# Experts of a mixture layer: the second product in four column quarters at once, the next expert's first product ahead of it, the sums by halves, the overflow path in the middle

## The chip, the cores and the metric

The kernel runs on one core of one Trainium2 chip. The metric is device time in microseconds (us) of one execution; the profile is of one execution of the same program. TensorE is the matrix engine (PE in the rows, PEld its weight loads), VectorE is DVE, ScalarE is ACT, GpSimd is POOL, and SyncE (SP) issues the weight loads.

## The reference

Two transformer blocks over 256 tokens of width 1024, all in float32. Block 1 is a mixer of gated linear attention and retention, followed by a mixture of 32 experts in 4 groups; block 2 has a gated recurrence mixer, two convolutional feed-forward layers and latent attention. The change is in the mixture of experts:

```python
def _hierarchical_moe(u, rg_w, rg_b, re_w, re_b, wg, wu, wd):
    ...
    g_idx = jnp.argmax(g_logits, axis=-1)
    ...
    top_v, top_i = lax.top_k(e_logits, TOP_K_IN_GROUP)
    weights = g_w * jax.nn.softmax(top_v, axis=-1)
    expert_ids = g_idx[:, None] * EXPERTS_PER_GROUP + top_i
    ...
    def run_block(args):
        e, tok, w = args
        xb = t[tok]
        hid = jax.nn.silu(xb @ wg[e]) * (xb @ wu[e])
        return ((hid @ wd[e]).astype(jnp.float32) * w[:, None])
    ...
    y = jnp.zeros((n, D), jnp.float32).at[slot_tok].add(outs.reshape(n_slots, D))
```

Each token goes to 2 of 32 experts. An expert's weights are two 1024 x 512 matrices (gate and up) and one 512 x 1024 matrix (down): 6 MiB, 192 MiB for all 32.

## The kernel before

All weights come through one stream of loads on SyncE's queue (`_load`, L302 to L309, issue line L306). One load fills one slot: a tile `w` of 128 x 2048 float32, 1 MiB. The slots are one pool (`sp`, tag "S") of `NS = 20`, and larger intermediate tensors (`x`, the hidden state of all tokens, among them) take slots of the same pool. `plan_loads` counts beforehand how many slots are alive at each point of the program and puts each load at the earliest point at which a slot is free, with two slots left over. Behind that, a load waits on the chip for what last used its slot, and for the load that went eight places ahead of it: the loads take eight completion semaphores in turn. Outside the experts every weight tile is split into a high and a low part (L324 on ScalarE, L325 on VectorE) and multiplied in three products (L359 to L361); the experts' weights are used as they come.

The mixture of experts is `moe` (from L982). After the routing, the experts are handled in 8 groups of 4; each expert has 32 token places (`CAP`). `moe_gather` (L1147) makes the token matrix of one group: 0/1 matrices on VectorE, 16 products `xg` (L1165), two scalings (L1168). `moe_weights` (L1172) makes `ct`, the weighted matrix from places to tokens. For each expert, `expert_hidden` (L1186) multiplies the 32 gathered tokens with the gate and up weights: for each of 8 row tiles, four products of 32 x 256 (L1193) that go to the four 32-column strips of the array and to the four 32-row strips of one bank `gu`. Then come Silu (L1196), the product with the up half (L1197), a transposition (L1198) and its copy (L1200). `expert_down` (L1203) multiplies with the down weights: two products of 32 x 512 for each of 4 row tiles (L1207), into rows 32 e to 32 e + 31 of two banks `ys`, so that all eight of an expert lie in the same 32-column strip. In the trace a float32 product is two matmul instructions. After the fourth expert of a group, `moe_combine` (L1210) copies the two banks to SBUF (L1215) and adds them to the tokens with four products (L1217) into four banks `acc`, which collect all 8 groups.

After the last group, `acc` is added to `x` (L1113) into `xn`. Then stands the overflow path: the largest number of tokens that any expert has (`ci`) is read into a register of every engine (L1118), and `If(n_max > CAP)` (L1119) encloses a loop that handles tokens beyond 32 places with weights loaded into two slots `ow`. With these inputs the path is skipped: the engines jump over it. Behind it, `hgrn` (from L1220) transposes `xn` (`tp`, L471), makes its high and low parts (L460, L462) and starts its first product `gf` (L359).

On each engine the instructions stand in one order, fixed when the program is built. What is inside the `If` is a unit of its own, and nothing moves from one side of it to the other.

## Time and profile before

| | |
|---|---|
| time, median of 3 runs | 1517.41 us (1516.98 to 1517.58) |
| span of the profiled execution | 1516.6 us, 0.8 us below the median |
| TensorE busy | 1435.2 us, 95% |
| VectorE busy | 792.6 us, 52% |
| ScalarE busy | 624.9 us, 41% |
| read from memory | 367.24 MB |
| experts: first product to last product | 414.4 to 870.1 us |

Matmuls are pipelined and their ends are modelled, so a busy TensorE is not TensorE at its peak. A wait is put down to what ended last. "SPq" is SyncE's queue: idle time there is a load that was held back. The times of the profiled execution count from its first instruction.

### The profile page before, as it was taken

The page shows a single profiled execution, that of the slowest core. Times are in us where ns is not written, and L with a number is a line of the kernel's source. Part 1 is how long each engine was busy: PE and PEld are TensorE (multiplying, and loading weights), DVE is VectorE, ACT ScalarE, POOL GpSimd, SP SyncE. Part 2 cuts the span into 40 slices and gives each one's busy share as a digit, 9 for nine tenths or more (in the row PEclk, how much of TensorE's full clock was granted, in tenths as well). Part 3 has the DMA queues.
Part 4 walks back from the last instruction along what each step waited for, and adds up shares of the span by engine and source line. Part 5 has one row for each costly group of instructions (what it writes and reads, how often), then busy time and mean ns, then how long its engine had stood idle before and what let it go on. Part 6 is the DMA issues. An engine that isn't in the chain of part 4 may idle for free. (4 is left out here: it accounts for less than half of the span.)

```text
span 1516.6 us, 24847 instructions
## 1 busy us (share of the span) xinstructions
PE 1435.2 (95%) x10158; PEld 1061.3 (70%) x10158; DVE 792.6 (52%) x1738; ACT 624.9 (41%) x1374; POOL 26.5 (2%) x31
## 2 busy tenths in 40 slices
PE   7999999999899988989989899999999998999998
PEld 7898878877743333333333298779999986799997
DVE  5987475655400000000000079878777767687794
ACT  5645444644200000000000085466656676565672
POOL 0000000000000000000000000000000001000000
PEclk9999999999899999999999999899999999999999
DMA  8335432586799999999999923456554214565500
GB/s 355 130 112 210 179 138 87 201 323 235 295 418 421 421 421 420 420 421 421 421 421 421 408 69 124 152 223 226 191 174 140 72 54 194 200 220 195 192 1 29
DMA packets 53529, 369.96 MB, mean 244 GB/s; under 512 B 6161, under 2 KB 7057, under 8 KB 9634
## 3 DMA queue, kind: packets, MB, share of 16 engines
q1 hardware_dynamic: 53410, 368.31, 62.1%
q8 instruction: 82, 1.34, 0.3%
q14 instruction: 37, 0.30, 0.1%
HBM read 367.24 MB, written 1.05 MB: 243 GB/s over the span
## 5 line engine op out<-in xcount | busy, mean ns | idle before, releaser
L325 DVE TENSOR_TENSOR wl<-w,wh 128x512 fp32r<-128x512 f32 (+2 forms) x644 | 403.9, 666 | 75.1 <-ACT wh L324 56.5
L324 ACT ACTIVATE wh<-w 128x512 fp32r<-128x512 f32 (+2 forms) x644 | 347.8, 613 | 158.6 <-PE u L360 65.8
L1207 PE MATMUL y<-w,t 128*32 128x512 f32 x512 | 227.4, 597 | 10.7 <-ACT t L1200 10.7
L359 PE MATMUL u<-xh,wh 128*128 128x256 f32 x704 | 199.4, 283 | 0.0
L360 PE MATMUL u<-xl,wh 128*128 128x256 f32 x704 | 199.2, 283 | 0.0
L361 PE MATMUL u<-xh,wl 128*128 128x256 f32 x704 | 199.1, 283 | 0.0
L1197 DVE TENSOR_TENSOR t<-t,gu 128x128 f32<-128x128 f32 x32 | 9.2, 288 | 315.5 <-ACT t L1196 315.5
L1207 PEld LDWEIGHTS y<-w,t 128*32 128x32 f32 x512 | 53.9, 110 | 160.7 <-issue 143.3
L1193 PE MATMUL gu<-w,t 128*32 128x256 f32 x2048 | 144.4, 382 | 0.0
L359 PE MATMUL gt<-wh,xh 128*128 128x512 f32 (+1 forms) x352 | 139.4, 396 | 0.0
L359 PEld LDWEIGHTS u<-xh,wh 128*128 128x128 f32 x704 | 134.9, 192 | 0.9
L360 PEld LDWEIGHTS u<-xl,wh 128*128 128x128 f32 x704 | 134.9, 192 | 0.8
L360 PE MATMUL gt<-wl,xh 128*128 128x512 f32 (+1 forms) x352 | 135.2, 384 | 0.0
L361 PE MATMUL gt<-wh,xl 128*128 128x512 f32 (+1 forms) x352 | 135.2, 384 | 0.0
L361 PEld LDWEIGHTS u<-xh,wl 128*128 128x128 f32 x704 | 134.9, 192 | 0.0
L1196 ACT ACTIVATE t<-gu 128x128 f32<-128x128 f32 x32 | 8.9, 278 | 252.2 <-PE gu L1193 252.2
L1193 PEld LDWEIGHTS gu<-w,t 128*32 128x32 f32 x2048 | 68.9, 109 | 56.9 <-issue 20.2
L359 PE MATMUL gf<-xh,wh 128*128 128x256 f32 x320 | 93.4, 292 | 1.7 <-ACT wh L324 1.7
L360 PE MATMUL gf<-xl,wh 128*128 128x256 f32 x320 | 91.9, 287 | 0.0
L361 PE MATMUL gf<-xh,wl 128*128 128x256 f32 x320 | 91.5, 287 | 0.0
L359 PEld LDWEIGHTS gt<-wh,xh 128*128 128x128 f32 x352 | 66.8, 190 | 12.8 <-ACT wh L324 0.5
L360 PEld LDWEIGHTS gt<-wl,xh 128*128 128x128 f32 x352 | 66.8, 190 | 12.9 <-issue 1.0
(394 smaller groups left out, 2144.8 us busy)
## 6 DMA issues: line engine op xcount, KB each, us to landing
w<-in_ex_gu SPq DMA_DIRECT2D x128, 1024.0 KB, 19.0
w<-in_ex_d SPq DMA_DIRECT2D x64, 1024.0 KB, 19.6
w<-in_w_in SPq DMA_DIRECT2D x44, 1024.0 KB, 5.4
w<-in_f_up SPq DMA_DIRECT2D x44, 1024.0 KB, 4.9
w<-in_f_dn SPq DMA_DIRECT2D x22, 1024.0 KB, 4.8
w<-in_hg_in SPq DMA_DIRECT2D x16, 1024.0 KB, 15.7
w<-in_br_ret SPq DMA_DIRECT2D x8, 1024.0 KB, 6.4
w<-in_br_gla SPq DMA_DIRECT2D x4, 1024.0 KB, 5.5
```

The lines of the kernel that those rows point to most:

```text
L324: self.nc.scalar.activation(h[:, a], r[:, a], AF.Copy)
L325: self.nc.vector.tensor_sub(l[:, a], r[:, a], h[:, a].bitcast(F32))
L359: mm(out, lh, rh, start=first, stop=False)
L360: mm(out, lh, rl, start=False, stop=False)
L361: mm(out, ll, rh, start=False, stop=last)
L1193: nc.tensor.matmul(b[32 * j:32 * j + 32, 0:256], xg[k // 4][:, (k % 4) * P + 32 * e:(k % 4) * P + 32 * e + 32], w[:, o:o + 256], start=k = ...
L1196: nc.scalar.activation(sg, b[:, 0:128], AF.Silu)
L1197: nc.vector.tensor_mul(hd, sg, b[:, 128:256])
L1207: self.nc.tensor.matmul(ys[c][32 * e:32 * e + 32, :], hT[:, 32 * j:32 * j + 32], ed[j // 2][:, o:o + 512], start=j == 0, stop=j == 3)
```

## The change

The second product is split by columns into four quarters of 256 instead of two halves of 512. For each row tile, the four quarters go to the four 32-row strips of one bank `y` and so to the four 32-column strips of the array, as the first product does. The strips are then copied to rows 32 e to 32 e + 31 of two SBUF tiles `Y`, two copies on VectorE and two on ScalarE for each expert; the copies of whole banks in `moe_combine` go. The transposition is a function of its own (`expert_turn`), and the second product of an expert is written behind the first product of the next one (`finish(prev)`); the stream of loads is ordered the same way. `moe_weights` moves to the end of its group. The sums over groups are made in two halves: groups 0 to 3 are added to `x` into `xn`, groups 4 to 7 to `xn`. The overflow path (`moe_rest`) stands between the halves, and takes three slots instead of two. The pool has 21 slots instead of 20, a pool of 512-wide tiles has 6 buffers instead of 5, and two 16-wide tiles have 2 buffers instead of 3. `x` is freed only at the end, so that `x` and `xn` are both alive in the second half. Comments and docstrings are gone throughout.

```diff
-NS = 20
+NS = 21
...
-    BUFS = {"t512": 5, "t384": 3, "t256": 7, "t128": 7}
+    BUFS = {"t512": 6, "t384": 3, "t256": 7, "t128": 7}
...
-        ms = self.small(16, "rsm", bufs=3)[:, :n]
+        ms = self.small(16, "rsm")[:, :n]
...
-        t = self.small(16, "rst", bufs=3)[:, :n]
+        t = self.small(16, "rst")[:, :n]
...
-        for e in range(NE):
-            for i in range(4):
-                self.add(("gu", e, i), A["ex_gu"][e, i], False)
-            for i in range(2):
-                self.add(("ed", e, i), A["ex_d"][e, i], False)
+        for e in range(NE + 1):
+            if e < NE:
+                for i in range(4):
+                    self.add(("gu", e, i), A["ex_gu"][e, i], False)
+            if e:
+                for i in range(2):
+                    self.add(("ed", e - 1, i), A["ex_d"][e - 1, i], False)
...
-        b = self.bank("cn")
-        mm(b[:, 0:32], one, A32[:, 0:32], start=True, stop=False)
-        mm(b[:, 0:32], one, A32[:, 32:64], start=False, stop=True)
-        cm, ci = sm(1), self.small(1, "ci", I32, bufs=1)
-        nc.vector.tensor_reduce(cm, b[:, 0:32], axis=AX.X, op=ALU.max)
-        nc.vector.tensor_copy(ci, cm)
-
-        nxt = (oh[1], self.moe_weights(oh[0], W3[:, :, 0:4]))
-        acc = [self.bank("cb") for _ in range(4)]
+        xn = None
+
+        def finish(last):
+
+            (g, e), hid, Y, oh = last
+            hT = self.expert_turn(*hid)
+            ed = [self.get(("ed", 4 * g + e, i)) for i in range(2)]
+            self.expert_down(hT, e, ed, Y)
+            self.free(*ed)
+            if e == 3:
+                ct = self.moe_weights(oh, W3[:, :, 4 * g:4 * g + 4])
+                self.moe_combine(ct, Y, acc, g % 4 == 0, g % 4 == 3)
+
+        nxt, prev = oh, None
         for g in range(8):
+            if g % 4 == 0:
+                acc = [self.bank("cb") for _ in range(4)]
             cur = nxt
-            ys = [self.bank("y"), self.bank("y")]
+            Y = [self.t512(), self.t512()]
             for e in range(4):
                 gu = [self.get(("gu", 4 * g + e, i)) for i in range(4)]
-                hT = self.expert_hidden(cur[0], e, gu.__getitem__)
+                hid = self.expert_hidden(cur[1], e, gu.__getitem__)
                 self.free(*gu)
-                ed = [self.get(("ed", 4 * g + e, i)) for i in range(2)]
-                self.expert_down(hT, e, ed, ys)
-                self.free(*ed)
-                if e == 1 and g < 7:
-                    a = slice(4 * g + 4, 4 * g + 8)
-                    oh = self.moe_gather(R3[:, :, a])
-                    nxt = (oh[1], self.moe_weights(oh[0], W3[:, :, a]))
-            self.moe_combine(cur[1], ys, acc, g == 0, g == 7)
-
-        xn = self.S("xn")
-        for c in range(2):
-            for t in range(2):
-                a = slice(t * D + c * 512, t * D + (c + 1) * 512)
-                nc.vector.tensor_add(xn[:, a], x[:, a], acc[2 * t + c])
-
-        ow = [self.S("ow") for _ in range(2)]
+                if prev:
+                    finish(prev)
+                prev = (g, e), hid, Y, cur[0]
+                if e == 1 and g % 4 < 3:
+                    nxt = self.moe_gather(R3[:, :, 4 * g + 4:4 * g + 8])
+            if g == 0:
+                b = self.bank("cn")
+                mm(b[:, 0:32], one, A32[:, 0:32], start=True, stop=False)
+                mm(b[:, 0:32], one, A32[:, 32:64], start=False, stop=True)
+                cm, ci = sm(1), self.small(1, "ci", I32, bufs=1)
+                nc.vector.tensor_reduce(cm, b[:, 0:32], axis=AX.X, op=ALU.max)
+                nc.vector.tensor_copy(ci, cm)
+            if g % 4 == 3:
+                finish(prev)
+                prev, base = None, xn or x
+                xn = xn or self.S("xn")
+                for c in range(2):
+                    for t in range(2):
+                        a = slice(t * D + c * 512, t * D + (c + 1) * 512)
+                        nc.vector.tensor_add(xn[:, a], base[:, a], acc[2 * t + c])
+            if g == 3:
+                self.moe_rest(nc.values_load(ci[0:1, 0:1], min_val=0, max_val=T), R32, W32, xn,
+                              [sm(n) for n in (64, 8, 8)])
+                nxt = self.moe_gather(R3[:, :, 16:20])
+        self.free(x)
+        self.x = xn
+
+    def moe_rest(self, n_max, R32, W32, xn, tmp):
+
+        nc, A = self.nc, self.A
+        ow = [self.S("ow") for _ in range(3)]
         for w in ow:
             nc.vector.memset(w[:, 0:1], 0.0)
-        n_max = nc.values_load(ci[0:1, 0:1], min_val=0, max_val=T)
+        q = [ow[2][:, i * 512:(i + 1) * 512] for i in range(4)]
         with self.tc.If(n_max > CAP):
+            Rr, Rg, Wg = tmp
+            nc.vector.tensor_copy(Rr, R32)
             with self.tc.For_i(1, T // CAP, 1):
-                nc.vector.tensor_scalar(R32, R32, -float(CAP), None, op0=ALU.add)
...
+                    oh, xg = self.moe_gather(Rg3, q[0:2])
+                    Y = q[2:4]
                     for e in range(4):
                         def load(name, i):
                             nc.gpsimd.dma_start(ow[i % 2], A[name][ds(g * 4 + e, 1), i].rearrange("o p f -> p (o f)"))
...
-                        hT = self.expert_hidden(oh[1], e, lambda i: load("ex_gu", i))
-                        self.expert_down(hT, e, [load("ex_d", i) for i in range(2)], ys)
-                    acc = [self.bank("cb") for _ in range(4)]
-                    self.moe_combine(ct, ys, acc, True, True)
+                        hT = self.expert_turn(*self.expert_hidden(xg, e, lambda i: load("ex_gu", i)))
+                        self.expert_down(hT, e, [load("ex_d", i) for i in range(2)], Y)
+                    ct = self.moe_weights(oh, Wg3)
                     for c in range(2):
+                        b2 = [self.bank("cb") for _ in range(2)]
                         for t in range(2):
+                            nc.tensor.matmul(b2[t], ct[:, t * P:(t + 1) * P], Y[c], start=True, stop=True)
                             a = slice(t * D + c * 512, t * D + (c + 1) * 512)
-                            nc.vector.tensor_add(xn[:, a], xn[:, a], acc[2 * t + c])
-        self.free(x, *ow)
...
+        return b, hd
+
+    def expert_turn(self, b, hd):
+        nc = self.nc
         nc.tensor.transpose(b[:, 256:384], hd, self.ident)
         hT = self.small(128, "t128")
         nc.scalar.copy(hT, b[:, 256:384])
         return hT
 
-    def expert_down(self, hT, e, ed, ys):
+    def expert_down(self, hT, e, ed, Y):
+
+        nc = self.nc
+        b = self.bank("y")
         for j in range(4):
-            for c in range(2):
-                o = (j % 2) * 1024 + c * 512
-                self.nc.tensor.matmul(ys[c][32 * e:32 * e + 32, :], hT[:, 32 * j:32 * j + 32],
-                                      ed[j // 2][:, o:o + 512], start=j == 0, stop=j == 3)
-
-    def moe_combine(self, ct, ys, acc, first, last):
-        """Four experts' outputs, weighted, to their tokens."""
-        nc = self.nc
+            for c in range(4):
+                o = (j % 2) * 1024 + c * 256
+                nc.tensor.matmul(b[32 * c:32 * c + 32, 0:256], hT[:, 32 * j:32 * j + 32], ed[j // 2][:, o:o + 256],
+                                 start=j == 0, stop=j == 3)
+        for c in range(4):
+            dst, src = Y[c // 2][32 * e:32 * e + 32, (c % 2) * 256:(c % 2 + 1) * 256], b[32 * c:32 * c + 32, 0:256]
+            if c % 2:
+                nc.scalar.copy(dst, src)
+            else:
+                nc.vector.tensor_copy(dst, src)
+
+    def moe_combine(self, ct, Y, acc, first, last):
+
         for c in range(2):
-            y = self.t512()
-            nc.scalar.copy(y, ys[c])
             for t in range(2):
-                nc.tensor.matmul(acc[2 * t + c], ct[:, t * P:(t + 1) * P], y, start=first, stop=last)
-
```

The order of the instructions follows from this code. TensorE at the first experts: `gu` is an expert's bank of the first product, `y` the second product, `w` the weight slots, `t` small tiles. Before:

```order
L1193 MATMUL gu_3752<-w_3250,t_477_3716 32x256 x8
L1193 MATMUL gu_3752<-w_3322,t_477_3716 32x256 x8
L1198 MATMUL gu_3752<-ident,t_491_3786 128x128
L1207 MATMUL y_3750<-w_3382,t_492_3790 32x512
L1207 MATMUL y_3751<-w_3382,t_492_3790 32x512
...
L1193 MATMUL gu_3812<-w_3448,t_475_3705 32x256 x8
```

And now, at the same place:

```order
L1217 MATMUL gu_3740<-w_3250,t_476_3699 32x256 x8
L1217 MATMUL gu_3740<-w_3252,t_476_3699 32x256 x8
L1217 MATMUL gu_3785<-w_3324,t_475_3698 32x256 x8
L1217 MATMUL gu_3785<-w_3384,t_475_3698 32x256 x8
L1217 MATMUL gu_3785<-w_3448,t_476_3699 32x256 x8
L1217 MATMUL gu_3785<-w_3450,t_476_3699 32x256 x8
L1226 MATMUL gu_3740<-ident,t_487_3774 128x128
L1238 MATMUL y_3833<-w_3452,t_495_3823 32x256 x8
L1238 MATMUL y_3833<-w_3454,t_495_3823 32x256 x8
```

The second expert's first product (`gu_3785`) has moved ahead of the first expert's transposition, and the second product is 16 products of 256 columns into one bank instead of 8 of 512 into two.

SyncE's queue at the middle of the experts, where the overflow path now stands. The names in brackets are what a load waits for: DMAHW0 to DMAHW7 are the eight completion semaphores, DMASW those of GpSimd's loads in the overflow path. Before, the same queue crosses the path among the loads of `hgrn`:

```order
L306 DMA w_5916<-in_hg_in 128x2048 [waits DMAHW7_49,PE_49]
L306 DMA w_5918<-in_hg_in 128x2048 [waits DMAHW0_49,PE_49]
L1118 TENSOR_LOAD ci_3735 [waits DVE_49]
L1119 COMPARE_AND_BRANCH
...
L1118 ISA x2
L306 DMA w_6399<-in_hg_in 128x2048 [waits DMAHW1_49,PE_49]
```

And now:

```order
L306 DMA w_4983<-in_ex_gu 128x2048 [waits DMAHW5_49,PE_49]
L306 DMA w_4985<-in_ex_gu 128x2048 [waits DMAHW6_49,PE_49]
L1130 TENSOR_LOAD ci_4031 [waits DVE_49]
L1143 COMPARE_AND_BRANCH
...
L1130 ISA x2
L306 DMA w_5448<-in_ex_d 128x2048 [waits DMAHW7_49,PE_49]
L306 DMA w_5450<-in_ex_d 128x2048 [waits DMAHW0_49,PE_49]
L306 DMA w_5452<-in_ex_gu 128x2048 [waits DMASW7_49,DMAHW1_49,DVE_49,PE_49]
L306 DMA w_5491<-in_ex_gu 128x2048 [waits DMAHW2_49,DMASW6_49]
L306 DMA w_5493<-in_ex_gu 128x2048 [waits DVE_49,DMAHW3_49,PE_49,Activation_49]
L306 DMA w_5495<-in_ex_gu 128x2048 [waits DMAHW4_49,PE_49]
```

The crossing has moved from behind the experts' last loads to the 110th of their 192 loads, which is the last gate and up load of the 19th expert; the two loads behind it take two slots that were left free, the next three the slots `ow`.

TensorE at the end of the experts: `cb` are the four products of `moe_combine`, `tp` the transpositions of `hgrn`. Before:

```order
L1217 MATMUL cb_3747<-t_892_5980,t_833_5618 128x512
L1217 MATMUL cb_3749<-t_892_5980,t_833_5618 128x512
L1118 TENSOR_LOAD ci_3735
L1119 COMPARE_AND_BRANCH
...
L1119 UNCONDITIONAL_BRANCH
L471 MATMUL tp_6324<-ident,xn_5984 128x128 x2
```

And now:

```order
L1238 MATMUL y_6711<-w_6543,t_944_6709 32x256 x8
L1204 MATMUL ct_6735<-ident,t_946_6732 128x128 x2
L1238 MATMUL y_6711<-w_6545,t_944_6709 32x256 x8
L1251 MATMUL cb_5442<-t_899_6410,t_948_6738 128x512
L1251 MATMUL cb_5444<-t_899_6410,t_948_6738 128x512
L1251 MATMUL cb_5443<-t_900_6411,t_948_6738 128x512
L1251 MATMUL cb_5445<-t_900_6411,t_948_6738 128x512
L471 MATMUL tp_6763<-ident,xn_5044 128x128 x2
```

The branch between the last sums and the first transposition is gone, and only half of the last expert's second product stands behind its last load (`w_6545`). Before and after the experts TensorE's rows are the same but for a few neighbours that changed places.

## Rows read from the trace of the kernel before

**Rows 1.** The page: busy time of TensorE.

```profile
PE 1435.2 (95%) x10158; PEld 1061.3 (70%) x10158; DVE 792.6 (52%) x1738; ACT 624.9 (41%) x1374; POOL 26.5 (2%) x31
```

**Rows 2.** Windows: busy per engine, granted clock, share of the DMA engines, GB/s.

```profile
430.00:850.00 420.00, 380.81 (x2650) 150.51 (x2651) 25.48 (x80) 27.13 (x81) 0.00 (x0) 1.00 1.01 421
```

**Rows 3.** Waits of TensorE from 430 to 850 us: total, times, longest.

```profile
PE gu L1198 <- DVE t L1197: 19.8, 26, 0.8
...
PE gu L1198 <- DMA w<-in_ex_gu: 1.6, 2, 0.8
```

**Rows 4.** Timeline of TensorE: start, length, line, tiles, count.

```profile
407.25 6.57 PE L1165 MATMUL xg<-t,x 128*128 128x128 f32 x32 [1.05 <-DVE t L1157]
413.66 0.31 PE L1085 MATMUL cn<-t,cst 128*128 128x32 f32 x2
...
414.37 3.66 PE L1193 MATMUL gu<-w,t 128*32 128x256 f32 x64
...
520.58 3.70 PE L1217 MATMUL cb<-t,t 128*128 128x512 f32 x8
...
528.65 0.33 PE L1198 MATMUL gu<-ident,t 128*128 128x128 f32 x1 [0.78 <-DVE t L1197]
...
859.37 7.05 PE L1207 MATMUL y<-w,t 128*32 128x512 f32 x16 [0.35 <-ACT t L1200]
```

**Rows 5.** Timeline of ScalarE: the first bank's copy in groups 1 and 2.

```profile
519.83 0.59 ACT L1215 COPY t<-y 128x512 f32<-128x512 f32 x1 [6.29 <-PE y L1207]
...
578.31 0.59 ACT L1215 COPY t<-y 128x512 f32<-128x512 f32 x1 [6.28 <-PE y L1207]
```

**Rows 6.** SyncE's issues: experts' loads 19, 20, 192, and eight later.

```profile
400.87 0.33 SPq L306 DMA_DIRECT2D w<-in_ex_gu  x1
415.50 0.33 SPq L306 DMA_DIRECT2D w<-in_ex_gu  x1
...
832.23 0.33 SPq L306 DMA_DIRECT2D w<-in_ex_d  x1
...
852.09 0.33 SPq L306 DMA_DIRECT2D w<-in_hg_in  x1
```

**Rows 7.** Waits on SyncE's queue from 430 to 850 us.

```profile
SPq L306 <- DMA w<-in_ex_gu: 161.2, 84, 3.4
```

**Rows 8.** Timeline at the end of the experts: TensorE, VectorE, ScalarE.

```profile
866.35 3.70 PE L1217 MATMUL cb<-t,t 128*128 128x512 f32 x8
...
870.09 0.69 DVE L1113 TENSOR_TENSOR xn<-x,cb 128x512 f32<-128x512 f32 x1 [0.17 <-PE cb L1217]
...
874.11 3.45 PE L471 MATMUL tp<-ident,xn 128*128 128x128 f32 x16 [4.06 <-PEq L1119]
...
874.81 0.90 ACT L460 ACTIVATE xh<-tp,wc 128x256 fp32r<-128x256 f32 x2 [7.76 <-PE tp L471]
...
879.10 0.36 PE L359 MATMUL gf<-xh,wh 128*128 128x256 f32 x1
```

**Rows 9.** The overflow path's branch (L1119): ns min/median/max, first and last start.

```profile
L1119 SPq COMPARE_BRANCH  x1: 50/50/50, 853.0 to 853.0; - x1
...
L1119 PEldq COMPARE_BRANCH  x1: 6103/6103/6103, 867.7 to 867.7; - x1
```

**Rows 10.** Copies on ScalarE out of PSUM: ns min/median/max.

```profile
L1200 ACT COPY t<-gu x32: 266/266/267, 419.1 to 859.1; 128x128 f32<-128x128 f32 x32
...
L1215 ACT COPY t<-y x16: 586/586/587, 463.6 to 866.5; 128x512 f32<-128x512 f32 x16
```

**Rows 11.** Windows ahead of the experts: TensorE busy, granted clock (third from the end).

```profile
400.00:405.00 5.00, 1.05 (x10) 0.97 (x9) 4.03 (x31) 0.97 (x3) 0.00 (x0) 0.78 1.01 421
405.00:410.00 5.00, 3.95 (x19) 3.82 (x20) 1.77 (x10) 0.00 (x0) 0.00 (x0) 0.50 0.98 411
410.00:412.50 2.50, 2.50 (x13) 2.50 (x13) 0.69 (x1) 0.00 (x0) 0.00 (x0) 0.50 0.03 13
```

**Rows 12.** TensorE's longest wait in total after the experts, 872 us to the end.

```profile
PE sd L565 <- DVE lv L541: 4.2, 4, 2.1
```

More of the change, by code (lines that the diff above doesn't have):

```diff
@@ L1159, in moe_gather @@
         wn = self.p("nffn")
-        xg = []
+        xg = xg or [self.t512() for _ in range(2)]
         for d0 in range(0, 8, 4):
@@ L1201, in expert_hidden @@
         return hT
-    def expert_down(self, hT, e, ed, ys):
+    def expert_down(self, hT, e, ed, Y):
+        nc = self.nc
+        b = self.bank("y")
         for j in range(4):
-            for c in range(2):
-                o = (j % 2) * 1024 + c * 512
-                self.nc.tensor.matmul(ys[c][32 * e:32 * e + 32, :], hT[:, 32 * j:32 * j + 32],
-                                      ed[j // 2][:, o:o + 512], start=j == 0, stop=j == 3)
-    def moe_combine(self, ct, ys, acc, first, last):
-        nc = self.nc
+            for c in range(4):
[9 more added lines that the diff above has]
+    def moe_combine(self, ct, Y, acc, first, last):
         for c in range(2):
-            y = self.t512()
-            nc.scalar.copy(y, ys[c])
             for t in range(2):
-                nc.tensor.matmul(acc[2 * t + c], ct[:, t * P:(t + 1) * P], y, start=first, stop=last)
+                self.nc.tensor.matmul(acc[2 * t + c], ct[:, t * P:(t + 1) * P], Y[c], start=first, stop=last)
     def hgrn(self):
```

15 lines of the change are left out of this document (6 added, 9 removed).

## The prediction

> **What bounds the kernel now.** I read the page first. TensorE is busy 1435.2 of 1516.6 us [rows 1], which invites the thought that any matmul time saved is time won. So I next cut out the stretch that the change touches, by windows. From 430 to 850 us TensorE is busy 381 of 420 us, but the DMA engines are busy all the time (share 1.01) at 421 GB/s [rows 2]. Two resources run near their limit together, and the question is which one waits. TensorE waited for a landing load 1.6 us in all of these 420 us; its larger wait is for VectorE inside an expert, 19.8 us [rows 3]. The loads waited for other loads, 161 us on the gate and up weights alone [rows 7], since each needs the one eight places ahead to have landed. So the loads do not starve TensorE, and they have no pause either.
>
> The rates show why. TensorE needs 58.5 us for a group of four experts (578.31 - 519.83) [rows 5]. The loads of a group are 24 tiles of 1.0486 MB; at 421 GB/s [rows 2] a tile is 2.49 us and a group 59.8 us. The two are within 1.3 us. TensorE begins at 414.4 with a store of tiles: the 19th load went out at 400.87 and the 20th had to wait until 415.50, when TensorE had freed the first slot [rows 6]. Because both run at one rate, most of that store is still unread at the end. The last expert load went out at 832.23, and the load eight places behind it, which needs its landing, at 852.09 [rows 6]: landed at 852.1. The last second product ends at 866.4 (859.37 + 7.05) [rows 4], 14.3 us later. That lag is what a faster TensorE can remove; the 437 us of loading are not.
>
> **The change, part by part.** *Second product.* An expert's 16 instructions of 512 columns take 7.05 us, 0.43 us each, one behind the other. The first product's 64 instructions of 256 columns, in the four strips, take 3.66 us, 0.057 us each [rows 4]. The new second product has that form: 32 x 0.057 = 1.8 us, 5.2 us less for each expert. An expert is then 3.7 + 0.3 + 1.8 = 5.8 us, the gather 6.6 us and the sums 3.7 us [rows 4]; with some 4 us of waits a group takes TensorE 38 us against 59.8 us of loads. The store is used up after about two groups, and from there each tile is multiplied as it lands. The 5.2 us are hidden behind the loads except at the end.
>
> *Start.* The count of tokens (0.3 us alone, at 413.66) and `ct` leave the path to the first product at 414.37 [rows 4]: 0.7 us. The 21st slot lets one more tile land before the experts start, one of 173 that took from 415.50 to 852.09 [rows 6]: 2.5 us. The last landing comes 3.2 us earlier, at 848.9. This needs the loads to stay without a pause.
>
> *Middle.* Let T be the landing of the 16th expert's last tile. Behind it SyncE has 10 more loads before the branch, then five into slots that are free or freed by the sums. The 16th load behind T needs a slot that the 17th expert's first product frees. TensorE ends its second product and copies at T + 2, the sums at T + 6.5 (4.4 us, below). Its branch took 6.1 us from 867.7, SyncE's 0.05 us [rows 9]; the gather is 6.6 us [rows 4]. So the slot is free at about T + 20. The 16th load may go when the 8th has landed, T + 20, and the DMA engines run dry only when the 15th has, T + 37. I price the middle at nothing: the eight loads in flight cover it, with 17 us to spare, and beyond that each us costs one. `xn` and the third slot `ow` leave at least 14 tiles ahead; eight fill the queue.
>
> *End.* After the last landing only half of one second product is left, 16 x 0.057 = 0.9 us, say 1.1 with its start, where 14.3 us stood: 13.2 us less. Behind it the copies of 32 x 256 are new, and no row has this shape. ScalarE's copies of 128 x 128 and 128 x 512 took 0.27 and 0.59 us [rows 10]; two in turn on each engine are 0.5 to 1.2 us, and I take 0.8, nearer to the small one as the rows are 256 long. With the hand-over that is 1.0. Products and sums then take what they took, 866.35 to 870.78, 4.4 us [rows 8]. Before, 4.4 us stood between the last second product and the end of the sums as well (866.4 to 870.8), since the first bank's copy overlapped it. So the end loses 1.0 us here.
>
> *The branch.* From the end of the sums (870.78) to the first `xh` (874.81) are 4.0 us, of which TensorE's branch explains the wait of 4.06 us [rows 8]. It goes. In its place ScalarE's `xh` stands behind one small operation on VectorE and one on ScalarE (the `lb` values, now after the sums), 0.7 us together by my guess from nothing to 1.5. Gain 3.3 us. From `xh` to the first `gf` (879.10) I leave the 4.3 us: the first tiles of `hg_in` land at about 851 and 854, well ahead.
>
> *Clock.* [...] Fed tile by tile, TensorE will have many short waits, and the clock may be low at the end. At that level the last half product, sums and transpositions would cost 0.9 + 3.7 + about 1 = 5.6 us more. With the clock high the sum is 3.2 + 13.2 - 1.0 + 3.3 = 18.7 us; low throughout, 13.1. I take 16.3, between the two, as no row shows this pattern. [...]
>
> *The rest.* Outside the experts TensorE's order is the same, and its largest wait there is 4.2 us [rows 12]: the extra slot and the two smaller buffers can move at most a few us, which I put at nothing, with 3 us either way.
>
> **The sum.** 1516.6 - 16.3 = 1500.3 us of span; the median stood 0.8 us above the span, so 1501 us.
>
> **The rivals.** *TensorE still behind at the end* (17%): the clock is low so often that TensorE enters the last group with a lag of half a group's gather and sums. Then the end gains 5 us rather than 13, and the time is 1509. For it: the low clock doubles a group to 76 us, more than the 59.8. Against: a TensorE that lags is busy without pause, and the fully busy stretch from 410 to 412.5 is the last one at the low level [rows 11].
>
> *Nothing* (6%): the loads bound before and after, so that neither product nor branch matters; 1514 to 1520. For it: the DMA engines are already full [rows 2]. Against: the 14.3 us between the last landing and the last product, and the branch, are no loading time.
>
> *Slower* (5%): the clock stays low through the experts. Eight groups at 76 us are 608 us where 456 stood (414.4 to 870.1), so about 1669 us. It decides from the point where a group takes more than 59.8 + 16.3 / 8 = 61.8 us, that is with the clock low for 63% of TensorE's work.
>
> *All of the saving counts* (1%): 32 x 5.2 = 166 us, 1351. It would need loads faster than the 421 GB/s.
>
> *The extra slot helps elsewhere too* (11%): loads in block 2 come earlier and a few us of TensorE's waits there go; 1495 to 1497.
>
> **How the numbers follow.** The case of the sum has 60%, at 1496 to 1506: its two clocks give 1498.7 and 1504.3, and 2 us for the rest. I widen to 1495 to 1509, which takes in the extra slot and a TensorE somewhat behind, and leaves out the tails on both sides. A difference under 0.2% (3 us) could not be told from no change. Faster: 60 + 17 + 11 + 1 = 89%; same 6%; slower 5%.
>
> **What would show it.** Right: DMA share 1.0 from 420 us on without a gap at the middle; TensorE's waits for the experts' loads grow from 2 us to over 100; the last `ed` tile lands near 849 and the sums end 6 to 10 us later; no wait on the branch ahead of `tp`; `gf` begins near 863. Wrong: a dip in GB/s where the branch now stands, second products longer than 2 us at the high clock, or an experts' stretch in which TensorE never waits for loads.

## The result, and the profile after

| | before | after |
|---|---|---|
| median of the runs, us | 1517.2 (1514.7 to 1517.6) | 1501.9 (1501.1 to 1504.2) |
| profiled execution: time, span, us | 1517.4, 1516.6 | 1504.2, 1502.5 |

The ratio is 0.9897, with a 95% interval from 0.988 to 0.9915: 15.3 us less, within the predicted range and 1 us above the predicted time. The profiled execution of after is the slowest of its four, 2.3 us above the median; where those microseconds lie is shown below.

Three views of after answer to [rows 1], [rows 2] and [rows 3]: the page's busy time, the windows, and TensorE's waits from 430 to 850 us (line, waited for: us in total, times, longest).

```profile
PE 1341.5 (89%) x10670; PEld 1040.7 (69%) x10670; DVE 822.4 (55%) x1807; ACT 637.4 (42%) x1423; POOL 26.5 (2%) x31
```

```profile
core 0: us, PE busy (x) PEld busy (x) DVE busy (x) ACT busy (x) POOL busy (x), PEclk, DMA share, GB/s
405.00:410.00 5.00, 2.02 (x8) 1.91 (x9) 3.87 (x28) 1.49 (x2) 0.00 (x0) 0.52 1.01 426
430.00:850.00 420.00, 303.22 (x3173) 134.32 (x3162) 53.16 (x149) 37.74 (x126) 0.00 (x0) 0.79 1.01 421
630.00:635.00 5.00, 2.79 (x13) 2.82 (x14) 1.43 (x7) 0.00 (x0) 0.00 (x0) 0.55 1.01 416
850.00:870.00 20.00, 15.56 (x118) 11.54 (x119) 13.65 (x31) 12.61 (x30) 0.00 (x0) 1.00 1.01 420
```

```profile
PE gu L1217 <- DMA w<-in_ex_gu: 64.5, 63, 2.7
PE y L1238 <- DMA w<-in_ex_d: 20.7, 18, 10.7
...
PE xg L1189 <- PEq L1143: 4.3, 1, 4.3
```

TensorE is busy 94 us less, and the time falls by 15. The stretch from 430 to 850 us is as full of loads as before, 421 GB/s; TensorE's busy time in it fell from 381 to 303 us, and waits for the experts' tiles, 85 us, stand where 1.6 us stood. The branch, now in the middle, holds TensorE 4.3 us, and the window from 630 to 635 us, in which it ends, shows no dip of the DMA engines: share 1.01, 416 GB/s.

The time was won behind the last landing. The timeline of the end, on SyncE, TensorE, VectorE and ScalarE (start, us, engine, line, what ended the idle time before), answers to [rows 6] and [rows 8]:

```profile
833.11 0.33 SPq L306 DMA_DIRECT2D w<-in_ex_d  x1
852.98 0.33 SPq L306 DMA_DIRECT2D w<-in_hg_in  x1
...
852.96 1.07 PE L1238 MATMUL y<-w,t 128*32 128x256 f32 x16 [0.96 <-DMA w<-in_ex_d]
854.96 3.70 PE L1251 MATMUL cb<-t,t 128*128 128x512 f32 x8 [0.93 <-ACT t L1243]
858.50 1.93 PE L471 MATMUL tp<-ident,xn 128*128 128x128 f32 x16
...
864.30 0.39 PE L359 MATMUL gf<-xh,wh 128*128 128x256 f32 x1 [0.50 <-ACT wh L324]
...
854.10 0.42 DVE L1245 COPY t<-y 32x256 f32<-32x256 f32 x1 [3.26 <-PE y L1238]
...
858.70 0.69 DVE L1128 TENSOR_TENSOR xn<-xn,cb 128x512 f32<-128x512 f32 x1 [0.17 <-PE cb L1251]
...
854.55 0.36 ACT L1243 COPY t<-y 32x256 f32<-32x256 f32 x1 [2.14 <-DVE t L1245]
...
860.70 1.57 ACT L460 ACTIVATE xh<-tp,wc 128x256 fp32r<-128x256 f32 x4 [1.00 <-DMA w<-in_hg_in]
```

The last expert load went out at 833.11; the issue eight places behind it, at 852.98, marks its landing. The last half product starts at that moment and ends at 854.03: a lag of 1.05 us where 14.3 stood. No wait on the branch stands ahead of `tp`. Block 2's first product `gf` starts at 864.30 instead of 879.10.

The start of an execution varies (`rk` starts between 403.9 and 407.5 us in four executions of what is one program up to there, below), so the terms are best counted from the routing's product `rk`, which comes ahead of all that was moved. It started at 404.75 before and at 406.94 after, as the timelines of TensorE show, first before, then after:

```profile
404.75 0.61 PE L1058 MATMUL rk<-t,cst 128*128 128x32 f32 x2 [3.95 <-issue]
...
406.94 0.61 PE L1060 MATMUL rk<-t,cst 128*128 128x32 f32 x2 [3.95 <-issue]
```

| stretch | before, us | after, us | won |
|---|---|---|---|
| `rk` to the last landing | 852.09 - 404.75 = 447.3 | 852.98 - 406.94 = 446.0 | 1.3 |
| last landing to end of the last second product | 14.3 | 1.05 | 13.3 |
| to the end of the sums | 4.4 | 859.39 - 854.03 = 5.4 | -1.0 |
| to the first `xh` | 4.0 | 860.70 - 859.39 = 1.3 | 2.7 |
| to the first `gf` | 4.3 | 3.6 | 0.7 |
| sum | 474.3 | 457.4 | 17.0 |

The start took 2.2 of these 17.0 us in this execution, and block 2, from `gf` to the end of the span, 0.7 (637.5 and 638.2), which leaves the 14.1 us by which the spans differ. Block 2 took 635.0 to 641.2 us in the fourteen profiles of this document, so a difference of a few us between two single executions can lie there.

### The profile page after: what moved, and what is told of

It is laid out like the page before. It is cut to its first block, busy times and chain, and to the rows that moved or that the text cites. A ratio compares the mean times of both kernels' runs of the same rounds, so it can differ in the third digit from the quotient of the medians.

```text
span 1502.5 us, 25968 instructions
## 1 busy us (share of the span) xinstructions
PE 1341.5 (89%) x10670; PEld 1040.7 (69%) x10670; DVE 822.4 (55%) x1807; ACT 637.4 (42%) x1423; POOL 26.5 (2%) x31
## 3 DMA queue, kind: packets, MB, share of 16 engines
HBM read 367.24 MB, written 1.05 MB: 245 GB/s over the span
## 4 chain that ended last, share of the span: by engine, by line
PE 54%; DMA 27%; DVE 8%; ACT 3%; issue 1%; POOL 0%; SPq 0%; ACTq 0%; POOLq 0%; DVEq 0%
DMA w<-in_ex_gu 19%; DMA w<-in_ex_d 7%; PE u L359 6%; PE u L360 6%; PE u L361 6%; PE gt L360 4%; PE gt L361 4%; PE gt L359 4%; PE acc L360 3%; PE acc L359 3%; PE acc L361 3%; DVE wl L325 3%; PE gu L1217 1%; PE op L359 1%; PE op L360 1%; PE op L361 1%
## 5 line engine op out<-in xcount | busy, mean ns | idle before, releaser
L1217 PE MATMUL gu<-w,t 128*32 128x256 f32 x2048 | 155.9, 446 | 65.7 <-DMA w<-in_ex_gu 64.5
L1217 PEld LDWEIGHTS gu<-w,t 128*32 128x32 f32 x2048 | 64.4, 122 | 154.0 <-DMA w<-in_ex_gu 102.6
L1238 PE MATMUL y<-w,t 128*32 128x256 f32 x1024 | 92.7, 500 | 25.1 <-DMA w<-in_ex_d 22.7
L1245 DVE COPY t<-y 32x256 f32<-32x256 f32 x64 | 26.8, 418 | 145.2 <-PE y L1238 132.2
L1243 ACT COPY t<-y 32x256 f32<-32x256 f32 x64 | 23.3, 364 | 136.7 <-DVE t L1245 136.7
L1238 PEld LDWEIGHTS y<-w,t 128*32 128x32 f32 x1024 | 33.8, 133 | 66.2 <-issue 32.4
```

What stands on the lines that cost most here:

```text
L1217: nc.tensor.matmul(b[32 * j:32 * j + 32, 0:256], xg[k // 4][:, (k % 4) * P + 32 * e:(k % 4) * P + 32 * e + 32], w[:, o:o + 256], start=k = ...
L1238: nc.tensor.matmul(b[32 * c:32 * c + 32, 0:256], hT[:, 32 * j:32 * j + 32], ed[j // 2][:, o:o + 256], start=j == 0, stop=j == 3)
L1243: nc.scalar.copy(dst, src)
L1245: nc.vector.tensor_copy(dst, src)
```

## Experiments

Twelve kernels ran, with four to ten measured executions each. The four of a batch ran on one chip beside the kernel before, whose medians were 1518.0, 1517.5 and 1518.5 us.

### The changed kernel once more

No edit. It is the anchor for the others, and tells whether the late start is the change's.

> The changed kernel once more, unaltered, as the anchor of this chip and for a second profile. Theory (the gain is the lag behind the last landing, some 13 us, plus some 3 us of branch): 1502 us. In the first profile the experts began 2.2 us later than before; if that was the start of that one execution (a load of the first block that landed 1.3 us later), this profile shows the first gather at about 405 us; if the change made it (smaller buffers, another order of loads), at 407 us again.

Measured: 1500.7 us (1499.6 to 1504.6), ratio 0.9882 (0.9864 to 0.9899). Its profile started late again, and so this run alone says nothing. Two kernels below, with the branch at the end and with the strips in turn, have the same instructions in the same order up to `rk` on every engine. The timeline at `rk` of the anchor:

```profile
407.54 0.61 PE L1060 MATMUL rk<-t,cst 128*128 128x32 f32 x2 [3.95 <-issue]
```

and of the kernel with the branch at the end:

```profile
403.86 0.60 PE L1060 MATMUL rk<-t,cst 128*128 128x32 f32 x2 [3.96 <-issue]
```

With the strips in turn (405.61) and the first profile of after (406.94) these are four executions of one and the same program up to there, and they reach `rk` between 403.9 and 407.5 us. The late start belongs to the execution, not to the change. Counted from `rk`, the anchor's last landing (853.23) comes after 445.7 us.

### Quarters, order ahead, neither

The second product's strips one after another, with the next expert's first product still ahead:

```
-        for j in range(4):
-            for c in range(4):
+        for c in range(4):
+            for j in range(4):
```

> The changed kernel with the second product one strip after another (the four instructions of a strip behind each other), so that its strips do not run at once; the next expert's first product still goes ahead. The second product should take about 6.9 us instead of 1.9. A group is then 4 x (3.7 + 6.9 + 0.3) + 6.6 + 3.7 + 0.3 = 54 us and about 1 of waits, 55, against 60 us of loads: eight groups end at 416 + 440 = 856, some 3 us behind the last landing. Theory (removed lag): 1505 us, with 1502 to 1508. Rival 1 (only the concurrent quarters remove the lag): 1514. Rival 2 (the branch is the whole gain): 1502, with no lag to be seen in the records of the end.

Measured: 1503.5 us (1503.2 to 1505.5), ratio 0.9901 (0.9886 to 0.9917). That is within the expected 1502 to 1508, but not for the expected reason: the second product took 4.7 us and not 6.9, as the third kernel of this section shows, so TensorE stayed well ahead of the loads. The lag was 4.6 us (856.21 - 851.62).

The quarters kept, each expert finished before the next one's first product, and the loads in that order:

```
-                if prev:
-                    finish(prev)
-                prev = (g, e), hid, Y, cur[0]
+                finish(((g, e), hid, Y, cur[0]))
```

> The changed kernel with each expert finished before the next one's first product, and the loads in that order; the quarters stay. TensorE then waits for the hidden values once for each expert, 1.2 us more of 32 times, so that a group is 38 + 5 = 43 us, still far under the 60 us of loads. Theory: 1502, the order ahead is worth nothing here. Rival (the order ahead carries the gain): 1507 or more.

Measured: 1500.8 us (1499.2 to 1504.1), ratio 0.9888 (0.9871 to 0.9905). The order ahead is worth nothing in the time beside the quarters, as the theory said, though the lag without it was 2.7 us (852.94 - 850.25).

Both edits at once:

> Both undone: the second product one strip after another and no first product ahead; the overflow path stays in the middle and the 21 slots stay. A group of TensorE is as long as before, 58.5 us, against 60 us of loads, so the store of tiles is not used up and the lag of some 13 us comes back. Theory: 1502 + 13 = 1515, with 1511 to 1516. Rival (branch and extra slot are the gain): 1502.

Measured: 1504.1 us (1502.3 to 1509.6), ratio 0.9903 (0.9887 to 0.9919), far from the 1515 expected. The edit did not do what it was meant to, as the timeline of this kernel shows (the 32 instructions of one product, and the landing and last product at the end):

```profile
501.41 1.05 PE L1233 MATMUL y<-w,t 128*32 128x256 f32 x4 [0.35 <-ACT t L1223]
502.76 3.71 PE L1233 MATMUL y<-w,t 128*32 128x256 f32 x28
...
853.77 0.33 SPq L306 DMA_DIRECT2D w<-in_hg_in  x1
...
854.79 4.09 PE L1233 MATMUL y<-w,t 128*32 128x256 f32 x28
```

Taken in turn, the strips still needed 4.7 us and not 6.9 (1.05 and 3.71, with two products `ct` between them). TensorE was faster than the loads: its last wait for one, 1.70 us, ended at 848.78, and it was in the first four instructions of the last product when the last tile landed at 853.77. What stands behind that, 5.1 us, is most of one product, since its first strip already needs both tiles. So this run tests no slow TensorE. It shows that a second product of 4.7 us is nearly as good as one of 1.9.

### The old second product in the changed kernel

The next two put the old product back, 16 instructions of 512 columns into the group's two banks with one copy each, everything else staying. First without the order ahead:

```
+        for j in range(4):
+            for c in range(2):
+                o = (j % 2) * 1024 + c * 512
+                self.nc.tensor.matmul(ys[c][32 * e:32 * e + 32, :], hT[:, 32 * j:32 * j + 32],
+                                      ed[j // 2][:, o:o + 512], start=j == 0, stop=j == 3)
```

> The changed kernel with the second product as it was before (16 instructions of 512 columns, 7.05 us, into the group's two banks, copied once for each group) and no first product ahead; overflow path in the middle, 21 slots and the sums by halves stay. The strips in turn took only 4.6 us a product, so that run left TensorE at 52 us a group; here it needs 58.5 again, against 60 us of loads, and the branch in the middle, which now has no idle time to hide in, costs it some 5 us more. Theory (the lag behind the last landing is set by TensorE's time for a group, and vanishes below some 55 us): the last second product ends near 871, gf begins near 880, 1517 us, with 1513 to 1519. Rival 1 (the branch's place and the slots are the gain): 1502 to 1505. Rival 2 (the lag comes back, and the branch's place still gains its 3 us): 1514.

Measured: 1513.9 us (1510.6 to 1518.2), ratio 0.9973 (0.9961 to 0.9984). Two groups' first copies on ScalarE, the last landing, the last product and the gather behind the branch in this kernel:

```profile
519.60 0.59 ACT L1240 COPY t<-y 128x512 f32<-128x512 f32 x1 [6.29 <-PE y L1234]
577.38 0.58 ACT L1240 COPY t<-y 128x512 f32<-128x512 f32 x1 [6.29 <-PE y L1234]
...
849.57 0.33 SPq L306 DMA_DIRECT2D w<-in_hg_in  x1
...
856.34 7.05 PE L1234 MATMUL y<-w,t 128*32 128x512 f32 x16 [0.35 <-ACT t L1227]
...
643.54 2.28 PE L1188 MATMUL xg<-t,x 128*128 128x128 f32 x19 [2.16 <-issue]
```

A group takes 57.8 us again and the lag is back: 863.39 - 849.57 = 13.8 us. The kernel with the quarters and no order ahead, 1500.8 us, differs from this one by the product and its copies alone: they are worth 13 us. This is the theory's mechanism, but rival 2's time. The branch in the middle did hold TensorE, for 4.25 us and then 2.16 us more within the gather. The two groups around it took 117.4 us where two others take 115.6, and from the first `gu` to the last product TensorE needed 449.4 us, no longer than the 452 before. Its `gf` started 6.4 us earlier than before and its span was only 2.7 shorter. Block 2 lost the rest; 2.3 us of it are one wait of TensorE (`sd`, L565) for nothing that the profile names, the others I have not followed.

Then with the order ahead:

> The changed kernel with the second product as it was before (7.05 us), and the next expert's first product still ahead of it. What goes is TensorE's wait for the hidden values, 19.8 us of seven groups, and the one for their transposed copy, 9.9 us: a group is some 54.3 us instead of 58.5. Theory: just below the knee, TensorE catches up with the loads near the end, and behind the last landing half an old product, 3.5 us, stands instead of 1.1: 1503.5 us, with 1502 to 1508. Rival (only the quarters remove the lag): 1513 or more.

Measured: 1509.8 us (1505.9 to 1512.7), ratio 0.9954 (0.994 to 0.9967), 6 us worse than expected. The timeline of this kernel, group, landing and the last two products:

```profile
520.29 0.59 ACT L1245 COPY t<-y 128x512 f32<-128x512 f32 x1 [5.86 <-PE y L1239]
576.09 0.59 ACT L1245 COPY t<-y 128x512 f32<-128x512 f32 x1 [5.86 <-PE y L1239]
...
850.18 0.33 SPq L306 DMA_DIRECT2D w<-in_hg_in  x1
...
842.69 13.87 PE L1239 MATMUL y<-w,t 128*32 128x512 f32 x32 [0.32 <-DMA w<-in_ex_d]
```

A group takes 55.8 us here, and TensorE catches up only in the last group. Then two old products, 13.87 us, stand one behind the other from 842.69 while their tiles land 5 us apart: the lag is 856.56 - 850.18 = 6.4 us and not 3.5. The group was expected at 54.3 us, and the branch in the middle, which the expectation left out, held TensorE for 4.25 and 2.41 us. The profiled execution is the fastest of five whose others reach 1512.7; why they spread I have not shown, and the lag of the others is not known.

### The branch at the end

```
-            if g == 3:
+            if g == 3:
+                nxt = self.moe_gather(R3[:, :, 16:20])
+            if g == 7:
                 self.moe_rest(
```

> The changed kernel with the overflow path's branch and its memsets behind the last sums again, instead of behind the first half's; all else stays. Theory: between the end of the sums and the first xh stand 4.0 us again instead of 1.3, and the middle gains nothing, since the loads hide it: 1502 + 2.7 = 1504.7, with 1503.5 to 1506. Rival (the branch's place is worth nothing): 1502. Rival (it is worth more, as the middle has a price): below 1502.

Measured: 1507.8 us (1506.5 to 1508.6), ratio 0.9938 (0.9924 to 0.9951), 6 to 7 us above the changed kernel and not 2.7. From its timeline the end of TensorE, and the branch on TensorE by its line (us at the end of the row):

```profile
851.40 5.40 PE L1252 MATMUL cb<-t,t 128*128 128x512 f32 x8 [0.93 <-ACT t L1244]
859.93 0.84 PE L471 MATMUL tp<-ident,xn 128*128 128x128 f32 x6 [3.13 <-DVEq L1144]
864.70 2.29 PE L471 MATMUL tp<-ident,xn 128*128 128x128 f32 x10 [3.93 <-issue]
...
L1144 PEldq COMPARE_BRANCH  x1: 6118/6118/6118, 852.9 to 852.9; - x1
```

The first pause is the known one. Behind six transpositions stands a second one of 3.93 us, in which TensorE waited for nothing that the profile names; before, all 16 ran through in 3.45 us. Up to `gf` this execution needs 465.6 us from `rk`, 8 more than the changed kernel (457.4 and 457.0): the sums took 1.7 us more (`cb` 5.40 for 3.70, at a granted clock of 0.64 from 853 to 856 us), the way to `xh` 1.5 and that from `xh` to `gf` 5.5, in which the second pause lies. Block 2 gave 3 us back (635.3 for 638.2). The last landing comes 849.42 - 403.86 = 445.6 us after `rk`, as with the branch in the middle (446.0 and 445.7): in the middle the branch cost the loads nothing.

### The kernel before with quarters alone

```
-            ys = [self.bank("y"), self.bank("y")]
+            Y = [self.t512(), self.t512()]
```

with the product and copies of the change and one more 512-wide buffer; slots, order and branch as before.

> The kernel before with one part of the change alone: the second product in quarters, with its copies. 20 slots, the old order and the branch at the end stay. Theory (parts add up): the lag behind the last landing falls from 14.3 to some 2.7 us, as in the changed kernel with none ahead, the copies take 1 us back, slot and branch are not gained: 1517.5 - 11.6 + 1 = 1507 us, with 1505 to 1511 (the run with the branch at the end cost 6 us where 2.7 were expected). Rival 1 (quarters are worth nothing without the rest): 1515 to 1518. Rival 2 (they are the whole gain): 1501.

Measured: 1511.4 us (1509.4 to 1513.2), ratio 0.9951 (0.9939 to 0.9964). The second pause again, in this kernel's timeline:

```profile
862.25 0.45 PE L471 MATMUL tp<-ident,xn 128*128 128x128 f32 x1 [4.29 <-PEq L1119]
867.74 3.36 PE L471 MATMUL tp<-ident,xn 128*128 128x128 f32 x15 [5.04 <-issue]
```

From `rk` to `gf` this execution is 5.1 us shorter than before (469.2 and 474.3), where 10.6 were expected. The second pause took 5.04 us, and the last landing came 1.0 us later (852.28 - 403.96 = 448.3), while the lag was 1.05 us and not the expected 2.7. So the parts don't simply add up: a branch behind the sums cost more here than before, when they ended 12 us later.

### Twenty slots

```
-NS = 21
+NS = 20
```

> The changed kernel with 20 slots instead of 21. Theory: one tile less has landed when the experts begin, and the last landing comes one tile's time, 2.5 us, later: 1502 + 2.5 = 1504.5, with 1503.5 to 1506. Rival (the slot is worth nothing): 1502. Rival (it helps block 2 too): above 1506.

Measured: 1504.1 us (1502.3 to 1505.7), ratio 0.9912 (0.9897 to 0.9927). Its routing and last landing:

```profile
405.27 0.61 PE L1060 MATMUL rk<-t,cst 128*128 128x32 f32 x2 [3.96 <-issue]
...
853.19 0.33 SPq L306 DMA_DIRECT2D w<-in_hg_in  x1
```

447.9 us from `rk` to the last landing, 1.9 to 2.2 more than with 21 slots: one tile's time, nearly.

### Half of the second matrix not loaded

One of an expert's two `ed` tiles is left out of the loads and the other read twice, in after and in before:

```
-            ed = [self.get(("ed", 4 * g + e, i)) for i in range(2)]
-            self.expert_down(hT, e, ed, Y)
+            ed = self.get(("ed", 4 * g + e, 0))
+            self.expert_down(hT, e, [ed, ed], Y)
```

> The changed kernel with one of the two tiles of an expert's second matrix left out of the loads; the second product reads the first tile twice, so TensorE's work is the same (the output is not the reference's). 32 tiles fewer of 2.49 us each. Theory (the loads bind in the changed kernel): a group is 20 tiles, 49.8 us of loads, still more than TensorE's 43, and the time falls by 32 x 2.49 = 80 us, to 1422, with 1418 to 1428. Rival (TensorE with its low clock binds, or is near it): 1440 or more.

Measured in after: 1423.6 us (1422.4 to 1424.8), ratio 0.9377 (0.9364 to 0.9389): 77 to 78 us less than the changed kernel, nearly all of the loading that was left out. The last landing came 366.2 us after `rk` instead of 446. Loads bind there from one end of the experts to the other.

> The kernel before with the same tile of each expert left out of the loads and the first one read twice; TensorE's work is the same (the output is not the reference's). Theory (before, TensorE with its 58.5 us a group sets the end, the loads only run beside it): the same 80 us of loading less is worth next to nothing, 1514 to 1518. Rival (the loads bind before as well): 1437 to 1470.

Measured in before: 1501.6 us (1497.5 to 1503.7), ratio 0.9878 (0.9862 to 0.9894). That is 17 us less, neither nothing nor 80. Two rows of a group's copies and a window of this kernel (columns as above):

```profile
520.03 0.59 ACT L1214 COPY t<-y 128x512 f32<-128x512 f32 x1 [6.29 <-PE y L1206]
575.95 0.59 ACT L1214 COPY t<-y 128x512 f32<-128x512 f32 x1 [6.29 <-PE y L1206]
...
600.00:650.00 50.00, 46.60 (x315) 17.39 (x314) 3.04 (x11) 3.54 (x11) 0.00 (x0) 1.00 0.93 374
```

The DMA engines now have pauses (0.93) and TensorE none for loads, so TensorE binds. But its group is 55.9 us instead of 58.5 [rows 5]: with other loads the scheduler had mixed the gather and the first products in another order, with fewer waits. From the first group's copy to the last group's it needs 386.3 us where before needs 402.0, and these 15.7 us are nearly all of the 17. The last tile landed at 819.73, 32 us ahead of the end of the last second product. TensorE had waited for loads only 1.6 us before [rows 3], so leaving them out could hardly give more than that directly; that the other order alone made the groups shorter is argued from the two timelines and not tested by itself. The edit had moved more than I meant it to, and the theory's number missed for that reason.

### A version that beats both

```
+        b2 = self.bank("fill")
+        for i in range(4):
+            self.pin(mm(b2, self.ident, x[:, i * 512:(i + 1) * 512], start=True, stop=True))
...
+        bs = [self.bank("y") for _ in range(2)]
```

and the small values `lb`, `om`, `wc` of block 2 are computed behind the routing's weights.

> The changed kernel with three small additions that the profile points to. Four products of 512 columns into an unused bank fill TensorE's idle 3.95 us during the routing, so that the granted clock stays high: the first gather should take 3.8 us instead of 6.3, and all loads behind the first freed slot come 2.4 us earlier. The small values for block 2 are computed during the routing instead of behind the last sums: 0.6 us less there. The four copies of the second product read two banks, one by each engine, and so run beside each other: 0.8 us less at the end. Theory: 3.8 us less than the changed kernel, 1497 to 1499. Rivals: the filler delays the routing or the clock falls anyway: 1500.5; if only the clock's term fails, the records show the gather at 6.3 us and the end 1.4 us shorter.

Measured: 1496.1 us (1494.6 to 1498.2), ratio 0.9853 (0.9836 to 0.9869); 5.9 and 4.7 us below the changed kernel's medians of 1501.9 and 1500.7, which ran on other chips, and 1 us below the expected 1497 to 1499. The window and the timeline of this kernel, and last the gather of the changed kernel:

```profile
405.00:410.00 5.00, 3.70 (x31) 3.59 (x32) 4.26 (x26) 1.49 (x2) 0.00 (x0) 1.00 1.01 428
```

```profile
401.17 3.68 PE L1004 MATMUL fill<-x,ident 128*128 128x512 f32 x8
405.25 0.41 PE L1063 MATMUL rk<-t,cst 128*128 128x32 f32 x2 [0.40 <-DVE t L1060]
...
407.16 3.84 PE L1206 MATMUL xg<-t,x 128*128 128x128 f32 x32 [1.05 <-DVE t L1198]
...
847.82 0.33 SPq L306 DMA_DIRECT2D w<-in_hg_in  x1
848.91 0.85 DVE L1262 COPY t<-y 32x256 f32<-32x256 f32 x2 [3.71 <-PE y L1255]
848.97 0.74 ACT L1260 COPY t<-y 32x256 f32<-32x256 f32 x2 [1.71 <-PE y L1255]
849.76 3.70 PE L1268 MATMUL cb<-t,t 128*128 128x512 f32 x8 [0.89 <-ACT t L1260]
853.75 3.03 ACT L460 ACTIVATE xh<-tp,wc 128x256 fp32r<-128x256 f32 x8 [4.04 <-PE tp L471]
...
409.45 6.68 PE L1189 MATMUL xg<-t,x 128*128 128x128 f32 x32 [1.05 <-DVE t L1181]
```

From 405 to 410 us the granted clock is 1.00 where it was 0.52, the gather takes 3.84 us instead of 6.68, and the last landing comes 847.82 - 405.25 = 442.6 us after `rk`, 3.1 to 3.4 earlier, where 2.4 were expected. `xh` starts before the sums end (854.19), 1.7 us earlier against them. The third addition failed: the copies do run beside each other, but the first `cb` waits for two of the four in either kernel, 0.93 us before and 0.89 now.

## Why the prediction was right, and where it was not

The predicted median was met, and its mechanism holds; two terms were off, and an argument behind it claimed more than it needed.

*What bounds the kernel.* Right, and tried from both sides: after, 80 us of loading less are worth 78; before, 17, of which TensorE's shorter groups hold 15.7, in a run in which it waits for no load. One reading on the way was not right: "most of that store is still unread at the end". At the last landing TensorE was still in the last but one expert's second product (its last expert's `gu` began at 852.59), so seven of the 19 tiles were left. The lag of 14.3 us does not hang on it.

*End.* Lag 14.3 to 1.1 predicted, 1.05 measured. With the old product put back it returned, 13.8 us, and 13 us of time with it (1500.8 to 1513.9).

*Second product.* The 1.9 us of 1.8 predicted are right, but a group of 38 us was never needed. Ordered by TensorE's time for a group, in kernels that all have the branch in the middle and 21 slots:

| second product | order ahead | group, us | lag, us | median, us |
|---|---|---|---|---|
| 7.05 us | no | 57.8 | 13.8 | 1513.9 |
| 7.05 us | yes | 55.8 | 6.4 | 1509.8 |
| 4.7 us | no | waits for loads | 5.1 | 1504.1 |
| 4.7 us | yes | waits for loads | 4.6 | 1503.5 |
| 1.9 us | no | waits for loads | 2.7 | 1500.8 |
| 1.9 us | yes | waits for loads | 1.05 | 1500.7, 1501.9 |

Of the 20 us that the prediction took off a group, the 2 us between the first two rows are enough for TensorE to catch up, if only in the last group. From there on a shorter product counts once, by what is left of it behind the last landing, and the order ahead no more than the runs can tell.

*Start.* Mis-sized: 3.2 us predicted, 1.3 and 1.7 measured from `rk`. The slot gave 1.9 to 2.2 of its 2.5. The step that failed is "The last landing comes 3.2 us earlier": the loads had no pause, but they were a little slower. From the first load that waited for a slot to the last landing it was 436.6 / 173 = 2.524 us a tile before and (852.98 - 417.19) / 172 = 2.534 after, which is 1.7 us over the stretch. With the old product and no order ahead the last landing came 849.57 - 405.31 = 444.3 us after `rk`, 3.0 earlier than before, nearly the predicted 3.2; so the loss came with the quick second product. Why a tile took 0.01 us longer then I have not shown.

*Middle.* Right. With the branch moved out of it the last landing came no earlier.

*Copies and sums.* Right, 1.0 us lost. The picture behind it was not: the two engines did not run in parallel but in turn, 0.42 and 0.36 us, each waiting for the other's, and `cb` waited for the first two alone.

*The branch.* 3.3 us predicted, 2.7 measured up to `xh`, and 0.7 more up to `gf`, where the prediction left the time as it was. Put back at the new end, it cost 6 to 7: two pauses, the second of which the prediction did not know, and in the profile also 1.7 us of low clock in the sums.

*Clock.* The step that failed is "I take 16.3, between the two": counted from `rk` the gain was 17.0, and the 850 to 870 window shows 1.00. Its lower case, 13.1, counts 5.6 us more for the half product, the sums and the transpositions at a low clock (0.50 in [rows 11]), an estimate that no run shows; in after they took 1.07, 3.70 and 1.93 us, at 1.00. The clock was low for part of the experts, as the prediction thought possible (0.79 from 430 to 850); TensorE still waited for loads there, 85 us, and no run shows a cost of it. The timeline of after shows three tiles of one expert:

```profile
838.06 1.07 PE L1217 MATMUL gu<-w,t 128*32 128x256 f32 x16 [1.41 <-DMA w<-in_ex_gu]
840.54 1.07 PE L1217 MATMUL gu<-w,t 128*32 128x256 f32 x16 [1.41 <-DMA w<-in_ex_gu]
843.01 1.93 PE L1217 MATMUL gu<-w,t 128*32 128x256 f32 x16 [1.40 <-DMA w<-in_ex_gu]
```

Equal waits of 1.4 us lie ahead of them. Two tiles took 1.07 us, at a granted clock of 1.00, and the third 1.93 us, at 0.50. Of the 82 tiles that TensorE waited for from 430 to 852 us, 37 took 1.07 us, 28 took 1.92 to 1.94 and 17 a time in between. The waits were 1.05 us on average (85.2 / 81). So the clock was low for a third of these tiles and not at the end; what decides which tile runs at which clock is not shown.

Whether the end falls into a good stretch is not fixed: with the branch at the end the last `cb` took 5.40 us (granted clock 0.64 from 853 to 856 us), where 3.70 stand here.

*The rest.* Right within its 3 us. The errors of Start and Clock nearly cancelled, and that is luck: the predicted number was closer than its terms.

*The signs.* Most came: DMA share 1.01, no wait on the branch ahead of `tp`, second products under 2 us, and, less the 2.2 us of the late start, `gf` at 862.1. TensorE's waits for loads grew to 85 us and not to over 100, since part of its 303 busy us ran at the low clock (0.79 on average). The last tile landed at 850.8 by the same count, and not near 849, which is the miss of Start.

The rivals: "still behind at the end" came to its time, 1509, in the kernel with old product and order ahead, but by the long product and not by the clock (granted clock 0.98 on average); in the changed kernel none of them did.

## What to carry to other kernels

Where a slower engine and a stream of loads run at nearly one rate, look at how far the engine lags behind the last landing. It must be fast enough to use up its store of tiles before the end: 58.5 us a group against 59.8 was not, 55.8 was in the last group, and a second product of 4.7 us was nearly as good as one of 1.9. What is won is that lag, once; after that the loads must start earlier or be fewer. Look for what delays the first freed slot, as a few microseconds there move the whole stream (with the first gather 2.8 us shorter the last landing came 3.1 to 3.4 us earlier). Count from an event that the change can't have touched, since an execution's start alone moved by 3.7 us here.

## What was not expected of the hardware

- Behind a skipped branch TensorE paused twice in four kernels: 3.1 and 3.9 us, 4.3 and 5.0 with the branch at the end, 4.25 and 2.16, 4.25 and 2.41 in the middle with the old product. Only the first is named by a wait. The DMA engines were full in every second pause (share 0.98 to 1.01). In before, with one pause of 4.06 us, their share was 0.49 from 870 to 874 us. With half of the second matrix not loaded in before it was 0.02; there the branch took TensorE 3.5 us instead of 6.1, and the one pause 1.56. So the branch was cheapest where no loads ran beside it, though no run changes that alone. The changed kernel paused only once, 4.3 us, with the engines full, so what decides the second pause stays open.
- Four products into a bank that nobody reads, in 3.95 us of idle time, kept the granted clock at 1.00, where 0.52 stood, and made the gather 2.8 us shorter (3.84 for 6.68); the last landing came 3.1 to 3.4 us earlier, counted from `rk`.
- Four strips taken in turn needed 0.13 us for an instruction of 256 columns (3.71 / 28), against 0.43 for one of 512 columns in a single strip [rows 4], half of which is 0.21. In the trace most of them start in pairs 0.01 us apart, all but the first four and the last four, as if two neighbouring strips ran at once; so they overlap more than the order of the program suggests.
- VectorE's and ScalarE's copies out of one bank ran in turn (0.42 and 0.36 us), each waiting for the other's, and those out of two banks side by side (two on each engine, 0.85 and 0.74 us). The waits between the copies are the program's own, so whether the two engines could read one bank at once is not shown.
